# Group norm on quarters of the PE array, and row sums of the spatial weights by halves

## The chip, the cores and the metric

The kernel runs on one core of one Trainium2 chip. The metric is the device time of one execution in microseconds (us). The kernel before took 996.74 us (median of three runs, 996.4 to 1000.49). The engines are named as in the profile: PE multiplies matrices (its weight loads are PEld), DVE is the vector engine, ACT the scalar engine, POOL the GpSimd engine and SP the engine that issues the DMAs. PE's clock has two levels, 1.2 and 2.4 GHz; a granted clock of 1.00 in a row is the upper one.

## The reference

The reference is one decoder block on 1024 tokens of width 1024. Two mixers stand side by side, a spatial gating unit (A) and a convolution branch (B), and a dense feed-forward part follows:

```
z = rmsnorm(x) modulated @ w_in + b_in;   u, v, val, gate = split(z)
y_a = gelu(u) * (tril(w_s) applied along each chunk of 128 tokens to layernorm(gelu(v)) + b_s)
y = depthwise causal conv, width 31, of val * sigmoid(gate), + bias
y_b = silu(layernorm of y over each of 8 groups of 64 channels, scaled by gn_g, shifted by gn_b)
x = x + gate1 * (concat(rmsnorm(y_a), rmsnorm(y_b)) @ w_out)
x = x + gate2 * ((silu(h2 @ wg) * (h2 @ wu)) @ w_ffn_out);   out = rmsnorm(x) modulated
```

The change touches the layer norm of branch B, called group norm below, and one term of branch A: since layernorm(v) has a shift, w_s applied to it needs the sum of each row of w_s times that shift, which the kernel folds into the bias b_s.

## The kernel before

Everything is held transposed: channels on the 128 partitions, tokens along the free axis, in two halves of 512 tokens. Most products are three matmuls (`mm3`, lines L603 to L605; `L928` in the feed-forward part): each operand is split into a high and a low part, and hi*hi, lo*hi and hi*lo are added in PSUM. The stages come in this order: norm of the first token half and adaLN; the gated projections `p` of half 0; `pu` and `v`; the spatial mixing `pm`; group norm of half 0; the same for half 1; the output projection `po`; then the feed-forward part in three rounds (`ah`, B and C banks) up to about 972 us; last the final norm and the output.

At the start, the squares `sq_n` are summed over channels by matmuls with 32 columns (`ssq_n`, L648: four of them, one for each quarter of the tokens), c is spread to all partitions (`c`, L538, two matmuls from one partition), silu of it is `cact` (L539), and DVE multiplies rows of the adaLN weights by `cact` and sums them (L559, on tiles called `ypad`, later `ada`) to get columns of `cond`. ACT finishes those columns (L722, L723); the first tile of activations is `t_h` on DVE (L725), `t_h` on ACT (L726), and `h` on ACT (L728, high part). The first gated product `p` (L603) needs `h`.

Group norm (`group_norm`, L881 on) runs four times, for two token halves times two pairs of channel tiles; each is called (half, pair) below, (0,0) to (1,1). A channel tile has 128 channels, so two groups of 64. Each run has these steps:
- L886: one fp32 matmul of 128 rows by 128 columns by 512 tokens for each tile, with the matrix `gcen` (identity less the mean over 64 channels), takes the mean away. `gcen` has nothing but zeros in two of its four quarters.
- L889, L890: ACT squares the result (`gsq`) and copies it back to `s`.
- L893: eight matmuls of 32 columns sum the squares by groups, for a quarter of the tokens (128) each, into one bank.
- L896, L897: ACT takes the root, DVE the reciprocal (`gsd`).
- L901: sixteen matmuls of 64 columns and 128 rows spread the factors over the channels.
- L904, L905: DVE multiplies, ACT applies silu with scale and shift.

The row sums of the spatial weights (`spatial_bias`, L698) are two fp32 matmuls against ones with 512 columns each, and eight DVE instructions (L707) on 64 partitions and 128 columns that add them into `bst`.

The order of all instructions on each engine is not the program's own: `fix_order` (L452) gives a list scheduler the whole program. It has a table of durations (`duration`, L125), a graph of dependences (`Graph`) and a simple clock of the engines (`Clock`, L313), which adds 0.09 and 0.12 us whenever PE goes to matmuls on a part of the array and back. It plans forward and backward a few times, takes the plan with the shortest modelled span, and fixes each engine's sequence. So a changed duration or a changed count of matmuls can move work anywhere in the program.

## Time and profile before

| | before |
|---|---|
| runs | 996.4, 996.74, 1000.49 us (median 996.74) |
| the profiled execution | 996.41 us, span in the trace 994.4 us |
| mean granted PE clock | 0.995 |
| PE busy | 961.9 us, 97% of the span, 4645 instructions |
| DVE busy | 855.2 us, 86% |
| ACT, POOL busy | 474.0 us (48%), 391.4 us (39%) |
| chain that ended last | PE 83%, DVE 10% |

The span runs from the first to the last instruction; the device time has 2.0 us beside it. A share of the span says how long an engine had work, not whether that work is on the chain that ends last; for this the windows and the timelines have to be read stage by stage. A PE matmul record lasts longer than its distance from the next one, since matmuls are pipelined: the cost of a matmul is read from start to start. A plain matmul of 512 columns starts 0.227 us after the one before. An fp32 matmul shows as two records.

### The profile page before, as it was taken

To read this page: it belongs to the slowest core of one execution; us is meant where nothing else is said; L and a number is where in the kernel's file an instruction comes from. 1 tells how busy PE (TensorE), PEld (TensorE's weight loads), DVE (VectorE), ACT (ScalarE), POOL (GpSimd) and SP (SyncE) were. 2 spreads that over 40 slices of the span, in tenths; PEclk is the share of its full clock that TensorE was granted. 3 is DMA by queue.
4 is the path that set the end of the run, shared out by engine and by line. 5 is a ranking of instruction groups with operands and counts; after the bars stand their busy time and mean duration, and the time that the engine had idled before them with its cause. 6 is when DMAs were issued, how large, how long until landed. Compare 5 with 4: busy or idle time off the path is not lost.

```text
span 994.4 us, 13218 instructions
## 1 busy us (share of the span) xinstructions
PE 961.9 (97%) x4645; PEld 773.6 (78%) x4645; DVE 855.2 (86%) x1197; ACT 474.0 (48%) x751; POOL 391.4 (39%) x232
## 2 busy tenths in 40 slices
PE   4999999999999999999999999999999999999994
PEld 2887777778878778888888877888887888888873
DVE  3969999999999444799999999998678989869946
ACT  6668467643484363564332332323337437236416
POOL 0037879755556111574445544445443100000121
PEclk9999999999999999999999999999999999999997
DMA  8983351524465515764677777677557838315104
GB/s 301 329 315 101 123 175 56 189 96 127 148 223 180 190 43 169 259 232 145 221 253 233 244 240 255 227 241 234 186 180 259 303 131 259 121 40 173 33 1 169
DMA packets 73667, 184.08 MB, mean 185 GB/s; under 512 B 8193, under 2 KB 10497, under 8 KB 73602
## 3 DMA queue, kind: packets, MB, share of 16 engines
q1 hardware_dynamic: 73602, 183.25, 55.6%
q8 instruction: 36, 0.59, 0.3%
q14 instruction: 29, 0.24, 0.1%
HBM read 142.06 MB, written 41.16 MB: 184 GB/s over the span
## 4 chain that ended last, share of the span: by engine, by line
PE 83%; DVE 10%; issue 2%; ACT 2%; DMA 1%; POOL 0%; SPq 0%; ACTq 0%; DVEq 0%; POOLq 0%
PE B L928 24%; PE C L928 14%; PE ah L928 11%; PE p L603 3%; PE po L603 3%; PE po L604 3%; PE po L605 3%; PE p L604 3%; PE p L605 3%; PE A L928 3%; DVE w_f L921 2%; PE v L604 2%; PE v L603 1%; PE pu L605 1%; PE v L605 1%
## 5 line engine op out<-in xcount | busy, mean ns | idle before, releaser
L928 PE MATMUL B<-h,w_f 128*128 128x512 f32 x816 | 190.8, 390 | 2.3 <-ACT x L1145 1.2
L928 PEld LDWEIGHTS B<-h,w_f 128*128 128x128 f32 x816 | 152.7, 188 | 36.4 <-DVE x L1147 3.1
L866 DVE SCALAR_TENSOR_TENSOR cv<-ypad,colt,cv 128x512 f32<-128x512 f32 x216 | 147.6, 745 | 0.5
L928 PE MATMUL B<-fa,w_d 128*128 128x512 f32 x528 | 125.5, 390 | 0.3 <-DVE x L1277 0.2
L928 PE MATMUL C<-h,w_f 128*128 128x512 f32 x528 | 123.6, 389 | 0.0
L928 PEld LDWEIGHTS B<-fa,w_d 128*128 128x128 f32 x528 | 98.8, 188 | 22.0 <-DVE x L1277 1.1
L928 PEld LDWEIGHTS C<-h,w_f 128*128 128x128 f32 x528 | 99.1, 188 | 20.6
L928 PE MATMUL ah<-h,wh_a 128*128 128x512 f32 x320 | 101.6, 395 | 0.5 <-ACT sg L673 0.5
L1209 POOL TENSOR_TENSOR sq_nf<-sq_nf,sq_nf 128x512 f32<-128x512 f32 x9 | 12.5, 1388 | 175.6 <-ACT sq_nf L1204 175.6
L920 ACT ACTIVATE w_d<-raw_d 128x512 fp32r<-128x512 f32 (+1 forms) x72 | 42.0, 593 | 83.0 <-PE B L928 34.0
L1170 POOL TENSOR_TENSOR x<-x,up 128x512 f32<-128x512 f32 x20 | 34.7, 1737 | 106.1 <-ACT x L1169 106.1
L587 POOL TENSOR_TENSOR wl_a<-raw_a,wh_a 128x1024 fp32r<-128x1024 f32 x20 | 49.2, 2461 | 67.8 <-ACT wh_a L586 57.7
L920 ACT ACTIVATE w_f<-raw_f 128x512 fp32r<-128x512 f32 x68 | 42.3, 627 | 68.4 <-PE B L928 41.6
L921 DVE TENSOR_TENSOR w_f<-raw_f,w_f 128x512 fp32r<-128x512 f32 x68 | 68.7, 1017 | 5.1 <-ACT w_f L920 5.0
L928 PEld LDWEIGHTS ah<-h,wh_a 128*128 128x128 f32 x320 | 59.9, 188 | 15.1 <-issue 1.4
L928 PE MATMUL C<-fa,w_d 128*128 128x512 f32 (+1 forms) x273 | 64.4, 384 | 0.0
L928 PE MATMUL ah<-h,wl_a 128*128 128x512 f32 x160 | 62.2, 390 | 0.0
L928 PEld LDWEIGHTS C<-fa,w_d 128*128 128x128 f32 x273 | 49.9, 188 | 11.0 <-issue 0.8
L921 DVE TENSOR_TENSOR fa<-a,fa 128x512 fp32r<-128x512 f32 x77 | 54.2, 743 | 1.7 <-ACT fa L920 1.7
L1277 DVE SCALAR_TENSOR_TENSOR x<-B,cond,x 128x512 f32<-128x512 f32 x48 | 35.6, 743 | 19.8 <-PE B L928 19.8
L920 ACT ACTIVATE fa<-a 128x512 fp32r<-128x512 f32 x77 | 46.0, 626 | 8.8 <-DMA a<-acts 5.7
L921 DVE TENSOR_TENSOR w_d<-raw_d,w_d 128x512 fp32r<-128x512 f32 (+1 forms) x72 | 47.8, 673 | 1.4 <-ACT w_d L920 1.4
(236 smaller groups left out, 2094.2 us busy)
## 6 DMA issues: line engine op xcount, KB each, us to landing
acts<-x SPq DMA_DIRECT2D x77, 256.0 KB, 3.1
a<-acts SPq DMA_DIRECT2D x77, 256.0 KB, 4.0
raw_f<-wf SPq DMA_DIRECT2D x32, 512.0 KB, 4.5
ada<-ada SPq DMA_DIRECT2D x24, 512.0 KB, 3.4
x<-ada SPq DMA_DIRECT2D x24, 512.0 KB, 3.8
raw_a<-wf SPq DMA_DIRECT2D x20, 512.0 KB, 3.8
ahead<-ahead SPq DMA_DIRECT2D x40, 256.0 KB, 3.0
ypad<-ada SPq DMA_DIRECT2D x16, 512.0 KB, 5.4
```

The lines of the kernel that those rows point to most:

```text
L587: lo_eng.tensor_tensor(lo, raw, hi.bitcast(F32), op=ALU.subtract)
L603: PE.matmul(acc, shi, mhi, start=start, stop=False)
L604: PE.matmul(acc, slo, mhi, start=False, stop=False)
L605: PE.matmul(acc, shi, mlo, start=False, stop=stop)
L866: V.scalar_tensor_tensor(accs[j], src, wc, accs[j], op0=ALU.mult, op1=ALU.add)
L920: A.activation(dst[:, 0, :], src, AF.Copy)
L921: lo_eng.tensor_tensor(dst[:, 1, :], src, dst[:, 0, :].bitcast(F32), op=ALU.subtract)
L928: last_mm = PE.matmul(bank[:, cols], s, m[:, cols], start=first and p == 0 and i == 0, stop=p == n - 1 and i == 2, skip_group_check=True)
L1170: G.tensor_tensor(g0, g0, up0, op=ALU.mult)
L1209: G.tensor_tensor(sums[half], sums[half], t, op=ALU.add)
L1277: V.scalar_tensor_tensor(xs[k][:, part], bank[:, cols], ccol(GATE2, k), xs[k][:, part], op0=ALU.mult, op1=ALU.add)
```

## The change

What the change does:
- L886: `gcen` is applied by its quarters. Each tile's matmul becomes two, each with 64 rows and 64 columns. The first tile's go on the two quarters of the array on the diagonal; the second tile's on the other two, so that its two halves of 64 channels come out exchanged. On the host the tables that belong to the second tile (group norm's scale and shift, the norm's gain, rows of `w_out`) are exchanged in the same way.
- L893: same number of matmuls; the layout of the sums in the bank is another, with each tile's sums on its own 64 partitions, and the order of the loop is another.
- L901: the sixteen spreading matmuls have 64 rows in place of 128, and their loop alternates between the two tiles.
- `spatial_bias`: two matmuls become eight of 64 columns and 128 tokens in one bank, and eight DVE instructions become four on 128 partitions.
- The planner: durations of an fp32 matmul in proportion to its columns and half as long with up to 64 rows; the matmuls of one PSUM bank stay in order; the clock of the forward plan runs PE at half speed when the stretch before was little used.

```
-            for hh in range(4):
...
+        rs = mm_bank("rs")
+        for hp in range(4):
+            for e in range(2):
+                PE.matmul(rs[e * 64:(e + 1) * 64, hp * P:(hp + 1) * P], ones.broadcast_to([P, 64]),
+                          wt[:, 2 * hp + e, :], start=True, stop=True)
+        for hp in range(4):
+            V.scalar_tensor_tensor(bst[:, hp, :], rs[:, hp * P:(hp + 1) * P], col("a_ln_b", hp),
+                                   bst[:, hp, :], op0=ALU.mult, op1=ALU.add)
...
-        for j in js:
-            PE.matmul(bank[j], gcen, s[j], start=True, stop=True)
+        for row in range(2):
+            for i, j in enumerate(js):
+                rows, outs = slice(row * 64, row * 64 + 64), slice((row ^ i) * 64, (row ^ i) * 64 + 64)
+                PE.matmul(bank[j][outs], gcen[rows, rows], s[j][rows], start=True, stop=True)
...
-        for i, j in enumerate(js):
-            for q in range(4):
-                PE.matmul(b0[q * 32:(q + 1) * 32, 0:P], gind[:, 32 * i:32 * i + 32],
-                          sqs[j][:, q * P:(q + 1) * P], start=i == 0, stop=i == 1)
+        for e in range(2):
+            for i, j in enumerate(js):
+                for b in range(2):
+                    o, q = 64 * i + 32 * b, 2 * b + e
+                    PE.matmul(b0[o:o + 32, 0:P], gind[:, 32 * e:32 * e + 32],
+                              sqs[j][:, q * P:(q + 1) * P], start=e == 0, stop=e == 1)
...
-        for i, (j, b) in enumerate(zip(js, (b1, b0))):
-            for q in range(4):
+        for q in range(4):
+            for i, b in enumerate((b1, b0)):
+                rows = slice(64 * i, 64 * i + 64)
                 for g in range(2):
                     PE.matmul(b[g * 64:(g + 1) * 64, q * P:(q + 1) * P],
-                              col("sel_grp", 8 * i + 2 * q + g).broadcast_to([P, 64]), sd,
+                              col("sel_grp", 2 * q + g)[rows].broadcast_to([64, 64]), sd[rows],
                               start=True, stop=True)
...
-        elif n == 128:
-            t = {128: 0.219, 32: 0.068}.get(m, 0.109)
         else:
-            t = 0.857
+            k = s.reads[0].box[1] - s.reads[0].box[0]
+            t = {128: 0.219, 32: 0.068}.get(m, 0.109 if k > 64 else 0.055) * n / 128
...
+            if s.engine == "PE":
+                if s.writes[0].name in bank:
+                    s.before.add(bank[s.writes[0].name])
+                bank[s.writes[0].name] = s.n
...
+        slow = 2 if self.throttled and self.active.get(w - 1, 0.0) < CLOCK_WINDOW / 2 else 1
```

What moves, at three places. In these rows a name ends in the number of its tile, and x2 or x4 counts equal instructions in a row; lines of the changed kernel are some 20 higher.

**The start.** PE of the kernel before, from the fifth sum of squares to the first two products:

```order
L648 MATMUL ssq_n1_0_119<-sq_n1_0_3_138,ones_92 32x128 x4
L648 MATMUL ssq_n1_0_119<-sq_n1_0_4_144,ones_92 32x128 x4
L538 MATMUL c0_97<-c_row_72,ones_92 128x512
L648 MATMUL ssq_n1_0_119<-sq_n1_0_5_150,ones_92 32x128 x4
L538 MATMUL c1_100<-c_row_72,ones_92 128x512
L648 MATMUL ssq_n1_0_119<-sq_n1_0_6_156,ones_92 32x128 x4
L648 MATMUL ssq_n1_0_119<-sq_n1_0_7_162,ones_92 32x128 x4
L654 MATMUL ssq_n1_0_119<-rt_n1_0_168,colt_74 128x128 x4
```

PE of the changed kernel at the same place:

```order
L669 MATMUL ssq_n1_0_119<-sq_n1_0_3_138,ones_92 32x128 x2
L559 MATMUL c0_97<-c_row_72,ones_92 128x512
L669 MATMUL ssq_n1_0_119<-sq_n1_0_3_138,ones_92 32x128 x2
L669 MATMUL ssq_n1_0_119<-sq_n1_0_4_144,ones_92 32x128 x4
L669 MATMUL ssq_n1_0_119<-sq_n1_0_5_150,ones_92 32x128 x4
L669 MATMUL ssq_n1_0_119<-sq_n1_0_6_156,ones_92 32x128 x4
L559 MATMUL c1_100<-c_row_72,ones_92 128x512
L669 MATMUL ssq_n1_0_119<-sq_n1_0_7_162,ones_92 32x128 x4
L675 MATMUL ssq_n1_0_119<-rt_n1_0_168,colt_74 128x128 x4
```

One more sum of squares (`sq_n1_0_6`) stands ahead of the second `c`, and the first `c` is two and a half sums earlier. ACT of the kernel before, from the first norm factor `r_n` on (`cond` with `gain` is L722, without it L723):

```order
L660 ACTIVATE r_n1_0_175<-ssq_n1_0_119 128x512
L722 ACTIVATE cond_105<-cond_105,gain_185,colt_74 128x1
L726 ACTIVATE t_h1_0_0_199<-t_h1_0_0_199,cond_105 128x512
L586 ACTIVATE wh_k1_235<-raw_k1_233 128x1024
L728 ACTIVATE h1_0_0_202<-t_h1_0_0_199 128x512
L723 ACTIVATE cond_105<-cond_105,colt_74 128x1
L726 ACTIVATE t_h1_0_1_241<-t_h1_0_1_241,cond_105 128x512
```

ACT of the changed kernel:

```order
L681 ACTIVATE r_n1_0_175<-ssq_n1_0_119 128x512
L741 ACTIVATE cond_105<-cond_105,gain_185,colt_74 128x1
L742 ACTIVATE cond_105<-cond_105,colt_74 128x1
L607 ACTIVATE wh_k1_235<-raw_k1_233 128x1024
L745 ACTIVATE t_h1_0_0_199<-t_h1_0_0_199,cond_105 128x512
L745 ACTIVATE t_h1_0_1_241<-t_h1_0_1_241,cond_105 128x512
L747 ACTIVATE h1_0_0_202<-t_h1_0_0_199 128x512
```

The second `cond` column, the next weights `wh_k1` and the second tile's `t_h` now all stand ahead of `h1_0_0`. DVE of the kernel before at that time:

```order
L559 SCALAR_TENSOR_TENSOR ypad2_108,cond_105<-ypad2_108,cact_96 128x1024
L725 TENSOR_TENSOR t_h1_0_0_199<-x0_76,r_n1_0_175 128x512
L559 SCALAR_TENSOR_TENSOR ypad3_109,cond_105<-ypad3_109,cact_96 128x1024
L725 TENSOR_TENSOR t_h1_0_1_241<-x1_77,r_n1_0_175 128x512
L725 TENSOR_TENSOR t_h1_0_2_283<-x2_78,r_n1_0_175 128x512
L729 TENSOR_TENSOR h1_0_0_202<-t_h1_0_0_199,h1_0_0_202 128x512
```

DVE of the changed kernel:

```order
L580 SCALAR_TENSOR_TENSOR ypad2_108,cond_105<-ypad2_108,cact_96 128x1024
L580 SCALAR_TENSOR_TENSOR ypad3_109,cond_105<-ypad3_109,cact_96 128x1024
L744 TENSOR_TENSOR t_h1_0_0_199<-x0_76,r_n1_0_175 128x512
L744 TENSOR_TENSOR t_h1_0_1_241<-x1_77,r_n1_0_175 128x512
L744 TENSOR_TENSOR t_h1_0_2_283<-x2_78,r_n1_0_175 128x512
L608 TENSOR_TENSOR wl_k1_236<-raw_k1_233,wh_k1_235 128x1024
L748 TENSOR_TENSOR h1_0_0_202<-t_h1_0_0_199,h1_0_0_202 128x512
```

The fourth `ypad` stands ahead of the first `t_h` where it stood behind it.

**Group norm (0,1).** PE of the kernel before, at the centring of the second pair of tiles (`gn0_2`, `gn0_3`):

```order
L605 MATMUL p11_0_1776<-h1_1_0_791,wh_vg11_0_1768 128x512
L603 MATMUL p11_0_1776<-h1_1_1_797,wh_vg11_0_1768 128x512
L886 MATMUL gn0_2_1553<-s0_2_1141,cstt_118 128x512
L886 MATMUL gn0_3_1554<-s0_3_1142,cstt_118 128x512
L604 MATMUL p11_0_1776<-h1_1_1_797,wl_vg11_0_1769 128x512
L605 MATMUL p11_0_1776<-h1_1_1_797,wh_vg11_0_1768 128x512
L603 MATMUL p11_0_1776<-h1_1_2_803,wh_vg11_0_1768 128x512
L893 MATMUL gn0_2_1553<-gsq0_2_1557,cstt_118 32x128 x4
L604 MATMUL p11_0_1776<-h1_1_2_803,wl_vg11_0_1769 128x512
L893 MATMUL gn0_2_1553<-gsq0_3_1560,cstt_118 32x128 x4
L605 MATMUL p11_0_1776<-h1_1_2_803,wh_vg11_0_1768 128x512
L603 MATMUL p11_0_1776<-h1_1_3_809,wh_vg11_0_1768 128x512
```

PE of the changed kernel (L907 is the centring, L916 the sums by groups, L787 the last matmul of `v`, L669 a sum of squares):

```order
L626 MATMUL v1_3_1429<-wl_v_3_992,h1_1_7_833 128x512
L907 MATMUL gn0_2_1556<-s0_2_1142,cstt_118 64x512 x2
L787 MATMUL v1_3_1429<-vb_116,vsel_117 128x512
L624 MATMUL p10_0_1746<-h1_1_0_791,wh_vg10_0_1738 128x512
L669 MATMUL ssq_a0_1599<-sq_a0_0_1600,ones_92 32x128 x4
L625 MATMUL p10_0_1746<-h1_1_0_791,wl_vg10_0_1739 128x512
L907 MATMUL gn0_3_1557<-s0_3_1143,cstt_118 64x512 x2
L626 MATMUL p10_0_1746<-h1_1_0_791,wh_vg10_0_1738 128x512
L624 MATMUL p10_0_1746<-h1_1_1_797,wh_vg10_0_1738 128x512
L916 MATMUL gn0_2_1556<-gsq0_2_1562,cstt_118 32x128 x2
L625 MATMUL p10_0_1746<-h1_1_1_797,wl_vg10_0_1739 128x512
L626 MATMUL p10_0_1746<-h1_1_1_797,wh_vg10_0_1738 128x512
```

The centring stands about 33 plain matmuls earlier, and its two pairs of quarters are no longer next to each other. In (0,0) all eight pieces are together and the spreading alternates between the tiles; in (1,0) the four quarters are together, and the spreading comes in two parts; in (1,1) the quarters are in two parts, and the spreading does one tile after the other. Counted over the program, PE goes to a block of matmuls on a part of the array 46 times where it went 37 times: group norm 19 for 11, row sums 1 for none, `pm` 6 for 7, the final norm 7 for 6.

**The end.** DVE of the kernel before (`x3` are the last products added to x, `rt_nf` the factors of the final norm, `of` output tiles):

```order
L1277 SCALAR_TENSOR_TENSOR x3_79<-C2_3_8208,cond_105,x3_79 128x256
L1244 SCALAR_TENSOR_TENSOR of0_4_8237<-x4_80,cond_105,ssq_nf0_8003 128x512
L1277 SCALAR_TENSOR_TENSOR x3_79<-C2_3_8208,cond_105,x3_79 128x256
L1226 RECIPROCAL rt_nf1_8269<-rt_nf1_8269 64x128
L1226 RECIPROCAL rt_nf2_8274<-rt_nf2_8274 64x128
L1244 SCALAR_TENSOR_TENSOR of0_6_8289<-x6_82,cond_105,ssq_nf0_8003 128x512
```

DVE of the changed kernel:

```order
L1302 SCALAR_TENSOR_TENSOR x3_79<-C2_3_8217,cond_105,x3_79 128x256
L1269 SCALAR_TENSOR_TENSOR of0_2_8242<-x2_78,cond_105,ssq_nf0_8012 128x512
L1269 SCALAR_TENSOR_TENSOR of0_4_8246<-x4_80,cond_105,ssq_nf0_8012 128x512
L1251 RECIPROCAL rt_nf1_8278<-rt_nf1_8278 64x128
L1302 SCALAR_TENSOR_TENSOR x3_79<-C2_3_8217,cond_105,x3_79 128x256
L1251 RECIPROCAL rt_nf2_8283<-rt_nf2_8283 64x128
L1269 SCALAR_TENSOR_TENSOR of0_6_8298<-x6_82,cond_105,ssq_nf0_8012 128x512
```

The first of the two reciprocals now stands ahead of the last product of `x3` where it stood behind it.

## Rows read from the trace of the kernel before

**Rows 1.** From the profile's page: busy time of PE and DVE, and the shares of the chain that ended last.
```profile
PE 961.9 (97%) x4645; PEld 773.6 (78%) x4645; DVE 855.2 (86%) x1197; ACT 474.0 (48%) x751; POOL 391.4 (39%) x232
...
PE 83%; DVE 10%; issue 2%; ACT 2%; DMA 1%; POOL 0%; SPq 0%; ACTq 0%; DVEq 0%; POOLq 0%
```
**Rows 2.** Busy time by stretches of the span: stretch, length, then for PE, PEld, DVE, ACT and POOL the busy us and instructions, the granted PE clock, DMA share, GB/s.
```profile
25.00:50.00 25.00, 25.00 (x106) 20.53 (x105) 25.00 (x38) 16.50 (x28) 0.00 (x0) 1.00 0.93 329
...
250.00:275.00 25.00, 25.00 (x134) 20.04 (x133) 24.62 (x36) 11.06 (x15) 13.91 (x7) 1.00 0.47 155
...
500.00:600.00 100.00, 99.81 (x438) 81.66 (x437) 99.98 (x127) 31.01 (x51) 49.68 (x29) 1.00 0.76 247
```
**Rows 3.** Timeline of PE at the start: start us, length, line, operation, shape, count [idle before, ended by].
```profile
8.57 1.30 PE L648 MATMUL ssq_n<-sq_n,ones 128*32 128x128 f32 x16 [1.59 <-ACT sq_n L641]
9.80 2.07 PE L538 MATMUL c<-c_row,ones 1*128 1x512 f32 x2
11.80 0.66 PE L648 MATMUL ssq_n<-sq_n,ones 128*32 128x128 f32 x8
12.39 2.07 PE L538 MATMUL c<-c_row,ones 1*128 1x512 f32 x2
...
24.22 0.80 PE L603 MATMUL p<-h,wh_k 128*128 128x512 f32 x1 [3.72 <-ACT h L728]
...
25.25 0.63 PE L603 MATMUL p<-h,wh_k 128*128 128x512 f32 x1
25.67 0.63 PE L604 MATMUL p<-h,wl_k 128*128 128x512 f32 x1
```
**Rows 4.** Timeline of ACT at the start.
```profile
21.89 0.81 ACT L726 ACTIVATE t_h<-t_h,cond 128x512 f32<-128x512 f32 x1 [0.29 <-DVE t_h L725]
22.61 1.04 ACT L586 ACTIVATE wh_k<-raw_k 128x1024 fp32r<-128x1024 f32 x1
23.56 0.61 ACT L728 ACTIVATE h<-t_h 128x512 fp32r<-128x512 f32 x1
24.08 0.28 ACT L723 ACTIVATE cond<-cond,colt 128x1 f32<-128x1 f32 x1
```
**Rows 5.** Timeline of DVE at the start.
```profile
19.95 1.22 DVE L559 SCALAR_TENSOR_TENSOR ypad<-ypad,cact 128x1024 f32<-128x1024 f32 x1
...
21.16 0.69 DVE L725 TENSOR_TENSOR t_h<-x,r_n 128x512 f32<-128x512 f32 x1
21.78 1.22 DVE L559 SCALAR_TENSOR_TENSOR ypad<-ypad,cact 128x1024 f32<-128x1024 f32 x1
```
**Rows 6.** Timeline of PE at the centring of (0,0): one plain matmul, the two fp32 matmuls of 128 by 128 by 512 (four records), and two plain ones, of which the first is left out.
```profile
141.66 0.39 PE L768 MATMUL v<-vb,vsel 128*128 128x512 f32 x1
141.90 1.88 PE L886 MATMUL gn<-s,cstt 128*128 128x512 f32 x4
...
143.85 0.40 PE L604 MATMUL v<-wh_v,h 128*128 128x512 f32 x1
```
**Rows 7.** Timeline of PE at the sums by groups of (0,0), eight matmuls of 32 columns (16 records) between plain ones, of which the first behind the block is left out.
```profile
144.08 0.40 PE L605 MATMUL v<-wl_v,h 128*128 128x512 f32 x1
144.41 0.64 PE L893 MATMUL gn<-gsq,cstt 128*32 128x128 f32 x16
...
145.32 0.40 PE L604 MATMUL v<-wh_v,h 128*128 128x512 f32 x1
```
**Rows 8.** Timeline of PE at the spreading of (0,0), sixteen matmuls of 64 columns in one block (32 records), and of (0,1), the first eight of them; the plain matmul right behind each block is left out.
```profile
153.06 0.39 PE L604 MATMUL v<-wh_v,h 128*128 128x512 f32 x1
153.38 1.97 PE L901 MATMUL gn<-gsd,colt 128*64 128x128 f32 x32
...
155.62 0.40 PE L603 MATMUL v<-wh_v,h 128*128 128x512 f32 x1
...
187.44 0.39 PE L604 MATMUL p<-h,wl_vg 128*128 128x512 f32 x1
187.76 1.09 PE L901 MATMUL gn<-gsd,colt 128*64 128x128 f32 x16
...
189.12 0.40 PE L603 MATMUL p<-h,wh_vg 128*128 128x512 f32 x1
```
**Rows 9.** Timelines at the row sums: PE's two fp32 matmuls between plain ones (the first one behind them is left out), then DVE's eight instructions.
```profile
117.13 0.39 PE L605 MATMUL pu<-h,wh_u 128*128 128x512 f32 x1
117.36 1.88 PE L702 MATMUL rs<-wt,ones 128*128 128x512 f32 x4
...
119.35 0.39 PE L604 MATMUL v<-wh_v,h 128*128 128x512 f32 x1
...
119.08 2.91 DVE L707 SCALAR_TENSOR_TENSOR bst<-rs,colt,bst 64x128 f32<-64x128 f32 x8
```
**Rows 10.** Timeline of DVE at the adding up for (0,1), the last step before its centring.
```profile
173.45 1.28 DVE L875 TENSOR_TENSOR s<-s,cv 128x512 f32<-128x512 f32 x2
```
**Rows 11.** Timeline of DVE at the end.
```profile
978.17 0.48 DVE L1277 SCALAR_TENSOR_TENSOR x<-C,cond,x 128x256 f32<-128x256 f32 x1 [1.17 <-PE C L928]
978.92 0.94 DVE L1226 RECIPROCAL rt_nf<-rt_nf 64x128 f32<-64x128 f32 x1 [0.26 <-ACT rt_nf L1225]
980.10 0.94 DVE L1226 RECIPROCAL rt_nf<-rt_nf 64x128 f32<-64x128 f32 x1 [0.24 <-ACT rt_nf L1225]
980.97 4.92 DVE L1244 SCALAR_TENSOR_TENSOR of<-x,cond,ssq_nf 128x512 f32<-128x512 f32 x11
```

More of the change, by code (lines that the diff above doesn't have):

```diff
@@ L176, in __init__ @@
         self.steps = []
-        uses, live, tiles, order = {}, {}, {}, {}
+        uses, live, tiles, order, bank = {}, {}, {}, {}, {}
         for ins in instructions:
@@ L319, in __init__, with tensor @@
         self.last, self.partial = None, False
+        self.throttled, self.active = throttled, {}
+    def tensor(self, t, s):
+        if s.partial != self.partial:
+            self.partial = s.partial
+            t += 0.09 if s.partial else 0.12
+        w = int(t / CLOCK_WINDOW)
+        slow = 2 if self.throttled and self.active.get(w - 1, 0.0) < CLOCK_WINDOW / 2 else 1
+        end = t + slow * s.issue
+        a = t
+        while a < end:
+            w = int(a / CLOCK_WINDOW + 1e-9)
+            b = min(end, (w + 1) * CLOCK_WINDOW)
+            self.active[w] = self.active.get(w, 0.0) + b - a
+            a = b
+        self.free["PE"] = end
+        return t, t + slow * s.finish
     def run(self, s, t):
@@ L405, in forward @@
             same = g.steps[n].engine == e and not s.dma
-            at[n] = max(at[n], (begin + s.issue if e == "PE" else end) if same else end + SIGNAL[e])
+            at[n] = max(at[n], (clock.free[e] if e == "PE" else end) if same else end + SIGNAL[e])
             if not need[n]:
@@ L1377 @@
     gind = np.zeros((P, 2, 32))
[L1378 to L1379 removed]
+    sel_grp = np.zeros((2, 2, 32, 4, 2))
+    for e in range(2):
         for g in range(2):
[L1381 to L1384 removed]
+            gind[part // 64 == g, e, 2 * e + g] = 1.0 / 64
+            for b in range(2):
+                sel_grp[:, b, 2 * e + g, 2 * b + e, g] = 1.0
+    colv.update(sel_tok=part[:, None] == 32 * np.arange(4)[None, :], sel_grp=sel_grp.reshape(P, 8),
                 sel_hl=((part == 0) | (part == 32))[:, None])
```

41 lines of the change are left out of this document (17 added, 24 removed).

## The prediction

> **What bounds the kernel now.** I read the page first. PE is busy 97% of the span and holds 83% of the chain that ended last; DVE holds 10% [rows 1]. Then the windows: in each of the ten stretches of 25 us from 25 to 275 us, whose first and last are shown, PE has no idle time (25.00 of 25.00), while DVE is full in some stretches only; between 500 and 600 us DVE is the fuller one, 99.98 to 99.81 [rows 2]. All that the change edits lies before 375 us: the row sums at 117, group norm at 142 to 190 and at 280 to 356. There every microsecond that PE needs more or less moves all that follows, and DVE's full stretch in the feed-forward part starts from results of PE, so it moves along. The two ends are latency: PE waits 3.7 us for the first `h` at 24.22 [rows 3], and the last DVE and output chain runs with PE idle [rows 11]. So the sum is made of PE's time in the edited blocks, and of shifts on the two ends. DVE's saving is left out of it, for the reason below.
>
> **Prices on PE.** They are read start to start, less 0.227 for each plain matmul in between. The two full centring matmuls cost 143.85 - 141.66 - 2 x 0.227 = 1.74, so 0.87 each [rows 6]. The eight group sums cost 145.32 - 144.08 - 0.45 = 0.79 [rows 7]. Sixteen spreading matmuls in one block cost 155.62 - 153.06 - 0.45 = 2.11, eight alone 189.12 - 187.44 - 0.45 = 1.23 [rows 8]. In a spreading block two matmuls of 64 columns run beside each other, one on each half of the columns; the second eight therefore add 0.88, about 0.11 for each matmul, and a visit to a block costs 1.23 - 0.88 = 0.35 beyond its matmuls. The group sums run four beside each other, so 0.79 is 0.35 and about 0.44. A visit thus costs 0.35, and this is paid for every block that the order makes, even a small one. Full matmuls like the old centring do not pay it.
>
> What no row shows is two matmuls on different halves of the rows beside each other. From below: they overlap in full, as column halves do; from above: one waits for the other. I take overlap, since the nearest rows are those of column tiles, and keep the other end as a rival.
>
> **Part by part, on PE, with overlap.**
> - Row sums: before 119.35 - 117.13 - 0.45 = 1.77 [rows 9]. After, eight matmuls of 64 columns with 128 rows are the half block of rows 8, so 1.23: -0.54.
> - (0,0), where the order keeps the four quarters together: centring 1.74 becomes one visit and one full length, 0.35 + 0.87 = 1.22. Group sums are now two blocks of two and six, 0.35 + 0.22 and 0.35 + 0.44 = 1.36 for 0.79. Spreading puts four beside each other: 0.35 + 0.88 = 1.23 for 2.11. Together 3.81 for 4.64: -0.8.
> - (0,1): centring in two blocks, 2 x 1.22 = 2.44 for 1.74; sums 1.36 for two blocks of 0.57 each, 1.14; spreading two blocks of eight as before, 2.46. Together 6.26 for 5.34: +0.9.
> - (1,0): centring 1.22 for 1.74, sums and spreading as before: -0.5.
> - (1,1): centring 2.44 for 1.74; sums 1.36 for 0.79; spreading does one tile after the other, so the row halves do not meet: 2.11 as before. +1.3.
> - One `pm` block fewer: -0.35.
>
> The sum is -0.54 - 0.8 + 0.9 - 0.5 + 1.3 - 0.35 = 0.0. What the quarters give in (0,0) and (1,0), the extra visits take in (0,1) and (1,1).
>
> **DVE.** Eight instructions of 2.91 us [rows 9] become four on twice the partitions, about 1.45. PE is full there and waits for nothing of DVE's, so this is worth nothing in time. It moves the adding up for (0,1) forward by about 1.5 us and a bit more from other orders, from 174.7 (173.45 + 1.28) [rows 10] to some 173. The centring that waits for it, however, is 33 plain matmuls earlier: 180.47 less 33 x 0.227 is 173. These two meet; a wait of 0 to 1 us is possible there, and behind it on PE all of the first `p` of the second half is queued. I take 0.
>
> **The start.** Ahead of the second `c` there is one more sum of squares, 0.6 us (11.80 to 12.39) [rows 3]: `c` starts at about 13.0, and all on DVE behind `cact` is 0.6 later, the third `ypad` at 20.55 instead of 19.95. One `ypad` takes 1.2 from start to start (19.95 to 21.16); the third and the fourth are now both ahead of the first `t_h`, which so starts at 22.95 rather than 21.16 [rows 5]. ACT now does the second `cond` column, which needs that `ypad`, then `wh_k1`, then two `t_h`, then `h`: 22.97 + 0.28 + 0.95 + 0.72 + 0.72 = 25.64, where `h` started at 23.56 [rows 4]. The first product follows 0.66 later, at 26.3 rather than 24.22 [rows 3]: +2.1. PE runs without a gap from here to 275 us [rows 2], so nothing takes this back. Cover for it could come only from matmuls that run faster: the first products start 0.43 apart (25.25 to 25.67) [rows 3], not 0.227, which is the pace of the lower of the two clock levels; that slow stretch begins with the first product, so I count it as moved as a whole. Bounds: 0 if the scheduled steps are not late in fact, 2.5 if a weight is late too.
>
> **The end.** DVE does the first reciprocal (0.87 start to start) ahead of the last product of `x3`. PE gives the sum that it needs 5 of 9 matmuls earlier, some 0.6, so the reciprocal starts at about 978.3 and the product at 979.2 in place of 978.17; from there the chain to the first output tile is the same (980.97 - 978.17 = 2.8), less 0.1 to 0.2 of a wait for ACT that falls away [rows 11]. The output chain starts 0.9 us later: +0.9, bounds 0 and 1.1.
>
> **Sum.** The profiled execution took 996.41 us (span 994.4, 2.0 beside it), the median of the runs 996.74. 996.4 + 0.0 + 0 + 2.1 + 0.9 = 999.4. That is 0.3% above the median, and by less than what can be told from no change.
>
> **A rule against it.** The rows show only matmuls on all rows or alone [rows 6 to 8], so none shows two row halves. The Trainium skill, page "TensorEngine Tiling (Array Packing)", section "Restrictions and Gotchas", says that tiles on different rows cannot access the same PSUM bank at the same time. No run before shows this. In (0,0) and (1,1) the first two quarters of a tile are on different rows and go to one bank, which is what the next rival takes up as a mechanism.
>
> **Rivals.**
> - *Row halves do not run beside each other (slower).* The place is L886 in all four runs and the spreading of (0,0). If the second quarter of a tile waits for the first one, each centring that is one full length above becomes two, in (0,0) four: 3 x 0.87 + 2 x 0.87 + 1 x 0.87 + 2 x 0.87 = 7.0, and the spreading of (0,0) 0.88 more; 999.4 + 7.9 = 1007. If only quarters that share a bank wait, (0,0) has three lengths and the spreading is spared: 2 + 2 + 1 + 2 = 7 lengths of 0.87, 6.1, so 1005.5. It decides from 2.3 us on, where the sum passes 1001.7. For it: no row shows the overlap. Against: column halves overlap in every block. Chance 0.2.
> - *The centring of (0,1) and the steps behind it wait (slower).* The order was made for a clock that is not the chip's; where DVE's adding up for (0,1) ends after PE is there, PE waits, and all of the first `p` behind it; up to 1 us there, and as much at each of the three steps behind it that hang on the same chain (sums, root, spreading): 1000.4 to 1003.4. For it: rows 10 and the meeting times above. Against: DVE gains 1.5 us. Chance 0.15.
> - *The quarters pay in full (faster).* The gain would be that of (0,0) in all four, 4 x 0.9 = 3.6 with 0.5 from row sums, and the start not late because the order shifts it back: 996.4 - 4 = 992.3; with gains in the rest of the order 989 to 992. For it: order of the feed-forward part also changes and its small PE waits can go. Against: the blocks are split in two runs, by the order. Chance 0.1.
> - *The change moves nothing.* The start and the end are as before in fact; 995.5 to 997. Chance 0.1.
>
> **How the numbers follow.** My forecast (997 to 1001.5) has 0.45. A change within 0.5% cannot be told from none here, that is 991.8 to 1001.7. Same: 0.45 + 0.1 (moves nothing) + 0.08 of the waits, which lie on both sides of 1001.7, + 0.04 of the full gain = 0.67. Slower: 0.2 + 0.07 of the waits = 0.27. Faster: the rest of the full gain, 0.06. The range leaves out the gains in full (0.1) and the upper part of the slower rival (0.08): 995 to 1006.5. Only the likeliest case alone: 997 to 1001.5.
>
> **What would show each step.** In the profile of the changed kernel: the first `p` at about 26.3 us, with `h` the releaser (start). The centring of (0,0) with four records started nearly together, and 1.2 us for the block (overlap); starts 0.43 apart pass after pass say that row halves wait. The spreading of (0,0) at 1.2 us with four records to a step. Blocks of two quarters in (0,1) at 1.2 us each. A wait of PE for `s` from DVE at the centring of (0,1). The first `of` of the last group about 1 us further from the last plain matmul. Wrong would be: a first `p` before 25.5, or a feed-forward part whose length differs by more than 1 us.

## The result and the profile after

The changed kernel took 999.75 us (median of 20 runs, 998.08 to 1002.63) beside 996.82 us for the kernel before (20 runs); the ratio is 1.0022, 95% interval 1.0012 to 1.0032. The forecast of 999.4 us held in its number. The slowdown of 0.1 to 0.3% lies inside the 0.5% that the prediction counted as no change, though over 20 runs it is clear of none. What follows shows that terms it did not have, of opposite sign, lie behind that number as well.

The page of the changed kernel's profile (profiled execution 1001.04 us, span 999.3, granted clock 0.992) has PE busy for 963.2 us, 96% of the span, and this chain, as in [rows 1]:

```profile
PE 87%; DVE 4%; ACT 3%; DMA 2%; issue 2%; POOL 1%; SPq 0%; ACTq 0%; DVEq 0%; POOLq 0%
```

**The start.** Timeline of PE, as [rows 3]:

```profile
9.78 2.07 PE L559 MATMUL c<-c_row,ones 1*128 1x512 f32 x2
11.78 1.92 PE L669 MATMUL ssq_n<-sq_n,ones 128*32 128x128 f32 x28
13.63 2.07 PE L559 MATMUL c<-c_row,ones 1*128 1x512 f32 x2
...
26.83 0.79 PE L624 MATMUL p<-h,wh_k 128*128 128x512 f32 x1 [5.09 <-ACT h L747]
```

of ACT, as [rows 4]:

```profile
23.60 0.29 ACT L742 ACTIVATE cond<-cond,colt 128x1 f32<-128x1 f32 x1 [0.76 <-DVE ypad L580]
23.80 1.04 ACT L607 ACTIVATE wh_k<-raw_k 128x1024 fp32r<-128x1024 f32 x1
24.75 1.50 ACT L745 ACTIVATE t_h<-t_h,cond 128x512 f32<-128x512 f32 x2
26.16 1.14 ACT L747 ACTIVATE h<-t_h 128x512 fp32r<-128x512 f32 x2
```

and of DVE, as [rows 5]:

```profile
22.34 1.22 DVE L580 SCALAR_TENSOR_TENSOR ypad<-ypad,cact 128x1024 f32<-128x1024 f32 x1
...
23.49 1.89 DVE L744 TENSOR_TENSOR t_h<-x,r_n 128x512 f32<-128x512 f32 x3
```

The chain is the predicted one, link by link: ACT waits 0.76 us for the fourth `ypad`, then come `cond`, the weights, two `t_h` and `h`. The wait for `h` grew from 3.72 to 5.09 us, by 1.37 where the sum had 1.5, and the first product starts at 26.83. The second `c`, though, starts 1.24 us later than before (13.63 for 12.39), not 0.6: between the two `c` there are now three and a half sums of squares (28 records, 8 before), and the first `c` starts no earlier than before (9.78 for 9.80), although two and a half sums fewer stand ahead of it.

**The blocks of group norm.** Timeline of PE: centring and spreading of (0,0), as [rows 6, 8], then the first of the two centring blocks of (0,1), and the spreading of (1,1):

```profile
145.37 0.40 PE L787 MATMUL v<-vb,vsel 128*128 128x512 f32 x1
145.70 1.09 PE L907 MATMUL gn<-s,cstt 64*64 64x512 f32 x8
146.72 0.50 PE L624 MATMUL v<-wh_v,h 128*128 128x512 f32 x1
147.05 0.40 PE L625 MATMUL v<-wh_v,h 128*128 128x512 f32 x1
...
155.04 0.39 PE L626 MATMUL v<-wl_v,h 128*128 128x512 f32 x1
155.36 1.10 PE L925 MATMUL gn<-gsd,colt 64*64 64x128 f32 x32
...
156.73 0.40 PE L625 MATMUL v<-wh_v,h 128*128 128x512 f32 x1
...
176.03 0.39 PE L626 MATMUL v<-wl_v,h 128*128 128x512 f32 x1
176.35 1.08 PE L907 MATMUL gn<-s,cstt 64*64 64x512 f32 x4
177.35 0.49 PE L787 MATMUL v<-vb,vsel 128*128 128x512 f32 x1
177.69 0.39 PE L624 MATMUL p<-h,wh_vg 128*128 128x512 f32 x1
...
358.27 0.39 PE L625 MATMUL po<-y_a,wl_o 128*128 128x512 f32 x1
358.59 1.59 PE L925 MATMUL gn<-gsd,colt 64*64 64x128 f32 x32
...
360.44 0.39 PE L624 MATMUL po<-y_a,wh_o 128*128 128x512 f32 x1
```

Read start to start, less two plain matmuls (0.45): eight records of four quarters cost 147.05 - 145.37 - 0.45 = 1.23 us, four records of two quarters 177.69 - 176.03 - 0.45 = 1.21, and 32 records of the spreading 156.73 - 155.04 - 0.45 = 1.24; in (1,1), where one tile follows the other, 360.44 - 358.27 - 0.45 = 1.72. Two quarters cost as much as four. This is what the prediction expects of row halves that run beside each other; experiment 5 takes up what else it could be.

**The end.** Timeline of DVE, as [rows 11]:

```profile
982.36 0.94 DVE L1251 RECIPROCAL rt_nf<-rt_nf 64x128 f32<-64x128 f32 x1 [1.04 <-ACT rt_nf L1250]
983.23 0.38 DVE L1302 SCALAR_TENSOR_TENSOR x<-C,cond,x 128x256 f32<-128x256 f32 x1
...
985.90 4.91 DVE L1269 SCALAR_TENSOR_TENSOR of<-x,cond,ssq_nf 128x512 f32<-128x512 f32 x11
```

The last product of `x3` stands behind the reciprocal and starts 0.87 later than that. It starts 0.80 us behind the last `C` product on PE (982.43), where it started 0.31 behind it before (977.86 and 978.17 in [rows 11]), and the output tiles 3.47 for 3.11: some 0.4 us. The other part of the end stands on PE: from the last `B` to the last `C` product it takes 12.53 us for 12.00, with a block of sums for the final norm (four records at 981.51) between the last `C` products, where it stood behind them.

**What the prediction did not have.** The table of PE's waits of the changed kernel (us in total, times, longest), some of its rows:

```profile
PE pu L624 <- ACT h L641: 1.3, 1, 1.3
PE ah L953 <- ACT sg L694: 1.2, 1, 1.2
PE B L953 <- DVE x L1172: 0.9, 2, 0.5
```

and the same table of the kernel before:

```profile
PE B L928 <- ACT x L1145: 1.2, 1, 1.2
PE B L928 <- DVE x L1147: 0.9, 1, 0.9
...
PE ah L928 <- ACT sg L673: 0.5, 1, 0.5
PE B L928 <- DVE x L1277: 0.2, 1, 0.2
```

The wait in `pu` is new; in the feed-forward part waits have gone. Where the first comes from is seen on the timelines of PE, DVE and ACT of the changed kernel, rows of all three in order of time:

```profile
95.66 0.39 PE L626 MATMUL pu<-h,wh_u 128*128 128x512 f32 x1
95.89 1.05 PE L675 MATMUL ssq_n<-rt_n,colt 128*128 128x128 f32 x8
96.98 0.75 DVE L636 SCALAR_TENSOR_TENSOR t_h<-x,cond,ssq_n 128x512 f32<-128x512 f32 x1 [0.92 <-PE ssq_n L675]
97.76 0.72 ACT L640 ACTIVATE t_h<-t_h,cond 128x512 f32<-128x512 f32 x1 [3.49 <-DVE t_h L636]
98.39 0.67 ACT L818 ACTIVATE ya<-pu,colt 128x512 f32<-128x512 f32 x1
98.96 0.62 ACT L641 ACTIVATE h<-t_h 128x512 fp32r<-128x512 f32 x1
99.63 0.50 PE L624 MATMUL pu<-h,wh_u 128*128 128x512 f32 x1 [1.30 <-ACT h L641]
```

PE spreads the norm factors of the second half (`ssq_n`) behind 26 products of `pu` in a row, and only six products stand behind it until the first that needs the new `h`. These cover 1.4 us, while `t_h`, another activation of ACT (`ya`) and `h` take 2.6 from the end of `ssq_n`. On DVE eight steps of the convolution stand ahead of the reciprocal that `ssq_n` needs, where three stood before, and it starts at 93.89 us for 90.52. But it is done at 94.83, and in this trace `ssq_n` follows the last product without a wait; in two later traces of this kernel it comes some 0.3 us late. So the order on PE and ACT makes most of this wait.

### The profile page after: what moved, and what is told of

Read it like the earlier page. It is cut to its first block, busy times and chain, and to the rows that moved or that the text cites. A ratio compares the mean times of both kernels' runs of the same rounds, so it can differ in the third digit from the quotient of the medians.

```text
span 999.3 us, 13264 instructions
## 1 busy us (share of the span) xinstructions
PE 963.2 (96%) x4673; PEld 773.2 (77%) x4673; DVE 862.6 (86%) x1193; ACT 476.4 (48%) x751; POOL 396.5 (40%) x232
## 4 chain that ended last, share of the span: by engine, by line
PE 87%; DVE 4%; ACT 3%; DMA 2%; issue 2%; POOL 1%; SPq 0%; ACTq 0%; DVEq 0%; POOLq 0%
PE B L953 28%; PE C L953 16%; PE ah L953 11%; PE A L953 3%; PE po L624 3%; PE po L625 3%; PE po L626 3%; PE p L624 2%; PE p L626 2%; PE p L625 2%; PE v L624 2%; PE v L626 2%; PE pu L624 1%; PE v L625 1%; PE pu L625 1%
## 5 line engine op out<-in xcount | busy, mean ns | idle before, releaser
L945 ACT ACTIVATE w_f<-raw_f 128x512 fp32r<-128x512 f32 x68 | 42.3, 628 | 72.3 <-PE B L953 39.5
```

Of the source, the lines that this page charges most:

```text
L945: A.activation(dst[:, 0, :], src, AF.Copy)
```

## Experiments

All ratios are to the kernel before, run beside them. Where the order of all else is said to be the same, every engine has the same sequence but for the instructions named.

**1. The planner's clock undone.**

```
-    slots, clock, table = Slots(g), Clock(True), None
+    slots, clock, table = Slots(g), Clock(), None
```

> The changed kernel with one line of the planner undone: its clock no longer runs PE at half speed after a little used stretch; everything else as changed. The order that comes out has the start and the end of the kernel before, the quarters of (0,1) in one block, the spreading of (0,1) in one block, and four pm blocks for six. My theory (PE blocks priced by visits, late start +2.1, late end +0.9, both from that one line): first product near 24.2 us, PE blocks 2.3 us cheaper than before the change (row sums -0.54, (0,0) -0.8, (0,1) -0.65, (1,0) -0.5, (1,1) +1.3, pm -1.05), so 994.5 us, ratio to before 0.998. Rival 1 (the group norm's own edits cost the time, the start is only noise of the DMA landing): 999 or more. Rival 2 (what is gained before 400 us is given back in the feed-forward part, where DVE is full): 996.5 to 997.

Measured 997.6 us (11 runs), ratio 1.000 (0.999 to 1.001). The late start and the late end are gone: PE waits 3.7 us for the first `h` as before, and from the last C product to the end of the span it takes 16.55 us, as before (16.57), where the changed kernel has 16.90. So in the changed kernel that one line makes the wait for `h` longer and the end late. It does not do so in every order: experiments 2 and 3 keep the line and have the wait of 5.1 us, but the end of before (16.6 and 16.5 us), and first products at 24.99 and 24.44, since their second `c` is not late. Added up on PE's timeline between plain matmuls, all blocks of fp32 matmuls up to the last one of group norm cost 38.7 us for 42.3 before, 3.6 less where the theory had 2.3. The time is 3 us above my theory's, and near rival 2's number, but from the first to the last B product this trace takes 516.0 us, not more than the 517.7 of before. Its trace has lost the rest ahead of the feed-forward part: PE waits 1.0 us for `sg` in `p` and a second time for `rt_n`, 1.4 us (a wait that one later trace of the kernel before has as well), and the clock fell after the wait for `y_b`, which experiments 7 and 8 take up.

**2. The planner's part alone**, with group norm and the row sums of the kernel before.

```
+            k = s.reads[0].box[1] - s.reads[0].box[0]
+            t = {128: 0.219, 32: 0.068}.get(m, 0.109 if k > 64 else 0.055) * n / 128
...
+                    s.before.add(bank[s.writes[0].name])
...
+    slots, clock, table = Slots(g), Clock(True), None
```

> The kernel before with only the planner's part of the change (durations, bank order, half-speed clock); group norm and row sums untouched. The order has the late start (fourth ypad ahead of the first t_h, two t_h ahead of h) but the second c where it was, and the end as before. My theory: first product +1.5 us, two pm blocks fewer and one group norm block more (-0.35), so 998.0, ratio 1.001. Rival 1 (the edits of group norm cost the time): 996.8. Rival 2 (the orders of the feed-forward part differ by more than all this): anything from 994 to 1001 with the first product at +1.5.

Measured 999.36 us (10 runs, 997.94 to 1004.8), ratio 1.0038 (1.0022 to 1.0054). The planner alone makes the kernel slower. The interval overlaps that of the whole change (1.0012 to 1.0032), so that the edits in group norm and the row sums give some of it back is not shown, and the edits under the old planner were not run. In its trace PE waits 5.09 us for the first `h`, as with the whole change, and the first product is at 24.99, +1.0 for the expected +1.5; ahead of the last group norm it has further waits, 1.2 us for `sg` in `pu`, 1.6 for a square `sq_n` and 0.5 for `s` in `pm`.

**3. The steps of group norm held together in blocks** (nine of the twelve in one, three still split once). Planner edges let the four quarters wait for both tiles and the eight sums for both squares, and hold the matmuls of a step in their own order:

```
+    def together(mms, ready=None):
+        edges.extend((m.name, ready.name) for m in mms if ready is not None)
+        edges.extend((b.name, a.name) for a, b in zip(mms, mms[1:]))
```

> The changed kernel with planner edges that make each group norm's four quarters wait for both tiles, its eight sums wait for both squares, and the spreading keep its alternating order, so that each step is one block in all four runs (three of the twelve are still split once). Planner's half-speed clock kept; the two c stand together early, so that the first product should come near 24.2. My theory: a step costs 1.22, 0.79 and 1.23 in one block, 3.24 a run for 4.6 to 5.3 before, with three splits at 0.35: PE blocks 6.5 us below the kernel before, so 990.3, ratio 0.9935. Rival 1 (visits are not the price, or the waits for the second tile take the place of what is saved): 997 to 999. Rival 2 (DVE's full stretch takes the gain back): 993 to 995.

Measured 993.09 us (6 runs), ratio 0.9962 (0.9948 to 0.9976). The direction held, the size did not: 3.9 us were gained of 6.5. The number is rival 2's, but not its mechanism: from the first to the last B product the trace takes 517.8 us, as before. In the trace the spreading of (1,1), which does one tile after the other in the changed kernel, is one block of four quarters at a time:

```profile
351.33 0.39 PE L625 MATMUL po<-y_a,wl_o 128*128 128x512 f32 x1
351.65 1.10 PE L934 MATMUL gn<-gsd,colt 64*64 64x128 f32 x32
...
353.02 0.40 PE L624 MATMUL po<-y_a,wh_o 128*128 128x512 f32 x1
```

353.02 - 351.33 - 0.45 = 1.24 us, and with the table further down: from the first product to the last matmul of group norm 328.0 us, for about 331.0 before, so 3 of the 6.5 us. The blocks themselves (group norm, row sums and `pm`, added up on PE's timeline) cost 26.6 us for 31.9, 5.3 less. Of that, waits for other engines take some: PE waits 1.5 us for `rt_b` where it waited 0.6, and 1.2 for `sg` where it waited 0.5. Where the rest goes is not shown.

**4. The same with the planner's clock undone.**

> As the gathered kernel, and with the planner's clock of the kernel before, so that the start and the end are those of before and pm has four blocks. My theory: PE blocks 7.2 us below the kernel before: 989.6, ratio 0.9928. Rival 1 (visits not the price): 996 to 997. Rival 2 (gain taken back by DVE's full stretch): 993 to 995.

Measured 994.85 us (12 runs), ratio 0.9974 (0.9962 to 0.9987): in rival 2's range, and not better than experiment 3. Here too the trace does not show rival 2's mechanism (517.1 us from the first to the last B product). All blocks of fp32 matmuls up to the last one of group norm cost 35.7 us for 42.3, 6.6 less; new waits take part of it, 1.7 us for `sg` in `p` and 1.5 for `rt_b` where it was 0.6, and in the profiled execution the clock fell behind the wait for `y_b`.

**5. The gathered kernel without the exchange of halves.**

```
-                rows, outs = slice(row * 64, row * 64 + 64), slice((row ^ i) * 64, (row ^ i) * 64 + 64)
+                rows, outs = slice(row * 64, row * 64 + 64), slice(row * 64, row * 64 + 64)
...
-        v = np.stack([v[:, 0], v[:, 1, ::-1]], axis=1).reshape((n * P,) + v.shape[4:])
+        v = np.stack([v[:, 0], v[:, 1]], axis=1).reshape((n * P,) + v.shape[4:])
```

> The gathered kernel with the second tile's halves not exchanged: both tiles' quarters lie on the diagonal of the array, and the tables on the host are left in their own order. The order of every engine's instructions is the same as in the gathered kernel. My theory (quarters run beside each other only where they are different quarters of the array): the first tile's quarter blocks the second's, the third quarter joins the second, so each centring block takes two to three lengths of 0.87 where it took one: 2.1 to 2.95 us for 1.22 in the trace, four times, so 3.5 to 7 us more on PE, of which some is given back later: 996 to 999 (gathered kernel 993.1). Rival (the four matmuls of a block were never beside each other, the gain came from the planner's order): same time, block length unchanged.

Measured 997.63 us (12 runs), ratio 0.999 (0.9974 to 1.0006) where the exchange gives 0.9962. Its centring block in (0,0):

```profile
142.39 0.40 PE L787 MATMUL v<-vb,vsel 128*128 128x512 f32 x1
142.72 1.94 PE L912 MATMUL gn<-s,cstt 64*64 64x512 f32 x8
...
144.93 0.39 PE L625 MATMUL v<-wh_v,h 128*128 128x512 f32 x1
```

144.93 - 142.39 - 0.45 = 2.09 us for 1.23 with the exchange: one length of 0.87 more, four times, 3.4 us. The same order of all instructions rules out that the order made the difference.

Two lengths, not three: in the program's order the second matmul of the block needs the quarter of the first, and the third a free one. If each started only after the one before it had, there would be three lengths, 2.96 us; so the third did not wait for the second.

One rival gives the same sums. If a matmul on 64 rows took half as long, as the planner's table now has it, and the row halves came one after the other, two quarters and four would cost 0.35 + 2 x 0.43 = 1.2 us, and the block without the exchange 0.35 + 4 x 0.43 = 2.1. The gathered kernel's trace decides: the centring of (1,1) is split there, one quarter alone (two records), then three.

```profile
342.93 1.07 PE L912 MATMUL gn<-s,cstt 64*64 64x512 f32 x2
343.92 0.50 PE L963 MATMUL ah<-h,wh_a 128*128 128x512 f32 x1
344.36 1.08 PE L912 MATMUL gn<-s,cstt 64*64 64x512 f32 x6
345.37 0.50 PE L963 MATMUL ah<-h,wh_a 128*128 128x512 f32 x1
```

From the start of the block to the next plain matmul it takes 0.99 us with one quarter and 1.01 with three, as it takes 1.00 with two (176.35 to 177.35) and 1.02 with four (145.70 to 146.72) in the changed kernel. One quarter takes the whole length, so the row halves do run beside each other. Quarters run beside each other only where they are different quarters.

**6. A known delay ahead of the feed-forward part.** In the kernel before, order of all else the same:

```
+            if half == 1 and ns == (7,):
+                for _ in range(22):
+                    EXTRA.add(PE.matmul(banks[7], unit(ws[7], 0)[0], full(yl[0])[0], start=True, stop=False,
+                                        skip_group_check=True).ins.name)
```

> The kernel before with 22 plain matmuls (22 x 0.227 = 5.0 us) added on PE just ahead of the last output projection of the second token half, at about 390 us; their results are overwritten by the next matmul, and the order of all other instructions on every engine is that of before. My theory after the first four runs (lateness at 409 us is given back in part by the feed-forward part, since about 0.28 of it was gone by 950 us in the five traces so far): +3.6 us at the end, 1000.5. Rival (the feed-forward part shifts as a whole, as the prediction had it; the differences between the traces came from other orders there): +5.0, 1002. Rival 2 (DVE's stretch does not depend on PE at all): +1 to +2.

Measured 1002.06 us (12 runs), ratio 1.0045 (1.003 to 1.006), so 3.0 to 6.0 us later. The first B product starts 4.97 us later than in the first trace of before, the last C product 5.68 later. The interval holds the theory's 3.6 as well as the rival's 5.0, so the times do not tell them apart. The trace speaks for the rival: from the first to the last B product it takes 518.4 us, inside the 517.6 to 519.5 of the other traces of before. The feed-forward part moves as a whole, as the prediction had it, as far as one trace can show; that it gives back 4 of 5 us is excluded.

**7. Zero matmuls in PE's wait for `y_b`**, in the changed kernel, order of all else the same but for the instruction that makes the zero:

```
+                    if half == 1 and part == 1 and n == 0:
+                        for _ in range(6):
+                            m = PE.matmul(banks[0], zero.broadcast_to([P, P]), full(yl[0])[0], start=False,
+                                          stop=False, skip_group_check=True).ins
...
```

> The changed kernel with six plain matmuls with a zero stationary operand (nothing is added to the result), in PE's wait of 1.57 us for y_b at 370 us; all other orders are the same but for one small ACT instruction at the start that makes the zero. In the changed kernel's trace the granted clock fell to 0.67 in 370 to 375 after that wait, and the po matmuls ran 0.43 apart; before the change it stayed at 1.00. Theory: with PE busy in the wait the clock stays at 1.00, po at 380 us comes 1.5 us earlier, the end about 1.1 earlier: 998.6. Rival (the fall has another cause, or it differs from run to run): the clock falls again, 999.7.

Measured 999.55 us (12 runs), ratio 1.0015 (1.000 to 1.003), not to be told from the 1.0022 without. The granted clock did stay at 1.00. The window of 365 to 375 us (PE busy, granted clock, DMA share, GB/s) in the changed kernel:

```profile
365.00:375.00 10.00, 7.62 (x35) 0.83 0.00 0
```

and in the one with the wait filled:

```profile
365.00:375.00 10.00, 9.01 (x48) 1.00 0.00 0
```

whose timeline of PE there is:

```profile
369.72 1.64 PE L947 MATMUL po<-y_a,zero 128*128 128x512 f32 x6
371.54 0.50 PE L631 MATMUL po<-y_b,wh_o 128*128 128x512 f32 x1 [0.18 <-ACT y_b L850]
```

In this trace the last `po` is 1.5 us earlier than in that of the changed kernel (406.90 for 408.40). The next run bears on why the median gains little: without filler, too, the clock does not fall every time.

**8. The kernel before again.**

> The kernel before once more, for a second trace: how far the landmarks move between two executions of one program (first product at 24.2, last product of the feed-forward part at 978). If the input's landing at the start or the clock after the wait at 366 us differ by 0.5 us or more here, differences of that size between other traces are no effect of the change. Expected: first product 24.2 to 24.9, clock 1.00 after the wait, 996 to 998.

Measured 1000.03 us in one run. The same order, the same wait of 1.50 us, and this time the clock falls, as the same window and the timeline of PE behind the wait show:

```profile
365.00:375.00 10.00, 8.50 (x33) 0.83 0.00 0
```

```profile
366.85 0.70 PE L603 MATMUL po<-y_b,wh_o 128*128 128x512 f32 x1 [1.50 <-ACT y_b L824]
367.35 0.63 PE L604 MATMUL po<-y_b,wl_o 128*128 128x512 f32 x1
367.78 0.63 PE L603 MATMUL po<-y_b,wh_o 128*128 128x512 f32 x1
```

The products start 0.43 apart, the pace of the lower of the two levels, and the landmarks behind are 1.6 us later. So this is no effect of the change: both kernels have it in some executions. Of the ten traces of this document in which PE waits 1.5 to 1.6 us for `y_b` without filler, the clock fell behind the wait in five.

**9. The gathered kernel with the wait filled** (the edits of 3 and 7).

> The gathered kernel with the six zero matmuls of the filled-wait kernel in PE's wait for y_b; the order of all else is that of the gathered kernel. Theory: blocks as in the gathered kernel (about 4 us below the kernel before), and the granted clock after the wait stays at 1.00 in every execution, where it fell in some of those without filler: ratio to before 0.9955 to 0.996, and a smaller spread of the single runs. Rival: the filler has no effect on the median, 0.9962 as without.

Measured 991.99 us (6 runs, 991.81 to 994.65), ratio 0.9961 (0.9948 to 0.9973). It beats both kernels, and is no better than experiment 3 by what can be told. In its trace the clock stayed at 1.00 behind the wait; with experiment 7 these are two traces, too few to show that the filler keeps it there.

**10 and 11. Both kernels again.**

> The changed kernel once more, for a second trace of the same order. Stage lengths to compare with the traces of before (three so far, 517.7, 519.5 and 518.4 us from the first B product to the last): if the changed kernel's feed-forward order is faster by itself, that length is again near 515 (515.2 and 514.4 in its two traces so far); if those were chance, 517 to 519. First product at 26.2 to 26.9, PE's wait for h in pu near 1.3 us, clock after the wait for y_b 1.00 or about 0.7, ratio 1.002 to 1.003.

> The kernel before a third time, beside the changed kernel in the same call: first B to last B product 517.5 to 519.5 us if its feed-forward order is slower by itself, near 515 if the length differs by chance. First product 23.9 to 24.9, 995 to 1000 us.

Measured 998.9 us (9 runs), ratio 1.0024 (1.0013 to 1.0035), for the changed kernel, and 998.08 in one run for the one before. The starts of five landmarks on PE and the end of the span, in us:

| trace | first p | last of group norm | first B | last B | last C | end |
|---|---|---|---|---|---|---|
| before | 24.22 | 355.08 | 448.22 | 965.87 | 977.86 | 994.43 |
| before again (8) | 23.93 | 355.29 | 450.01 | 969.51 | 981.51 | 998.08 |
| before again (11) | 23.73 | 356.91 | 450.10 | 967.65 | 979.64 | 996.22 |
| before and delay (6) | 24.21 | 355.01 | 453.19 | 971.55 | 983.54 | 1000.11 |
| changed | 26.83 | 359.91 | 454.71 | 969.90 | 982.43 | 999.33 |
| changed again (10) | 26.30 | 360.39 | 453.66 | 966.77 | 979.30 | 996.20 |
| changed, filled (7) | 26.35 | 359.89 | 453.18 | 967.61 | 980.13 | 997.82 |
| gathered (3) | 24.44 | 352.48 | 445.50 | 963.26 | 975.26 | 991.78 |

From first to last B the order of before takes 517.7, 519.5, 517.6 and 518.4 us, the changed order 515.2, 513.1 and 514.4. The same number of matmuls stands between the two landmarks. Within one order the length moves by some 2 us (the gathered kernel and experiment 5 have one order, and take 517.8 and 515.6), but the two sets do not touch, and side by side, in experiments 10 and 11, they are 4.4 us apart: the feed-forward part of the changed order is some 4.0 us shorter by itself (means 518.3 and 514.2). Experiment 6 shows that this is not because it starts later: 5 us later, the order of before still takes 518.4.

## Why the prediction was right, point by point

- **Blocks on PE (predicted 0.0 in all).** The prices hold to a few hundredths: one visit and one length 1.23 for 1.22, the spreading of (0,0) 1.24 for 1.23, two quarters alone 1.21. One was too high: two tiles' spreading one after the other in (1,1) cost 1.72, not 2.11, so the row halves meet in part there. Added up on PE's timeline between plain matmuls, group norm, row sums and `pm` cost 31.3 us for 31.9 before, so -0.6 for the predicted 0.0.
- **Row halves beside each other.** The step that no row of before showed, and the rival that hung on it, are settled by the blocks above and by experiment 5 with the single quarter shown there: they run beside each other, and matmuls on the same quarter do not. The rule of the Trainium skill that the prediction weighed (page "TensorEngine Tiling (Array Packing)", section "Restrictions and Gotchas": tiles on different rows can't access one PSUM bank at the same time) does not agree: in (0,1) two quarters on different rows write different partitions of one bank, and the block takes 1.21 us, not 2.1. The measurement decides.
- **The start (predicted +2.1).** Measured: the means of the first product are 24.02 (four traces of before's order) and 26.49 (three of the changed order), so +2.5. The links are those that were named; mis-sized was the second `c`, 1.24 us late in the first trace for 0.6. Experiment 1 shows that the planner's clock is the cause of the longer wait for `h`; how late `c` comes is another matter of the order (experiments 2 and 3). The first products start 0.43 apart in the traces of both kernels, so the slow stretch did move along, as the prediction took it.
- **The end (predicted +0.9).** Last B to last C 12.53 us for 12.00, and last C to the end 16.90 for 16.57, so +0.86 in two of the three traces; in the third, that of experiment 7, the last C to the end takes 17.69. The number fits, the reason in part: the reciprocal gives some 0.4 of it. The other 0.5 is the added block of the final norm on PE (7 for 6 in the count of blocks), which the sum left out, though it had a price for it, 0.35.
- **"PE runs without a gap from here to 275 us, so nothing takes this back."** This failed. The changed order itself has a gap there, 1.30 us in `pu`, since six products cover the 2.6 us until the second half's first `h` only in part. I had read the windows of before, and not looked for what the new order puts around the second half's norm. With 0.7 more for `sg` in `ah` that is +2.0 that the sum did not have. From the first product to the last matmul of group norm the changed kernel takes 333.6 us (mean of three), the one before 331.0 (its three traces without the one that waits 1.6 us for `rt_n` a second time; 331.5 with it): +2.6 or +2.0.
- **The centring of (0,1) waits (a rival, 0.15).** It did not: the changed kernel's table of waits has no wait of PE for `s` there, and 176.35 follows 176.03 as in the other blocks.
- **"DVE's full stretch moves along."** As to lateness this was right (experiment 6). But the sum took the feed-forward part's order as equal, and it was 4.0 us shorter: a term that I set to zero without costing it. The prediction had named a length that differs by more than 1 us as a sign that it is wrong, and by this sign it is. In the four traces of the order of before, the waits of B for `x` and of C for `fa` add up to 2.3, 4.3, 2.8 and 3.3 us; in the three of the changed order to 0.9, 0.3 and 0.9. That is 2.5 of the 4.0. Which step on DVE made them shorter I have not shown.

Together, with +0.2 from the last matmul of group norm to the first B: +2.5 + 2.6 + 0.2 - 4.0 + 0.5 + 0.6 = +2.4 by the means of the traces (+1.8 with all four of the order of before; the delay of experiment 6 is taken off), beside +2.9 and +1.9 in two sets of medians. The number of the forecast, +2.6 to 3.0, came out because the missed terms, +2.0 and -4.0, and the 0.4 by which the start was short, cancel in good part. The prices of the blocks, the links of the start and half of the end were right; that the middle came to no more than this was not reasoned, and was luck.

## What to carry to other kernels

Pricing a block of small matmuls needs two numbers, its lengths and the visits (0.35 us each here): an edit that halves the lengths and lets a scheduler split the blocks comes out even, and the same edit with the blocks held together gave 0.4%. When a planner writes the order, a changed cost model is an edit of its own, and must be timed alone (here 1.0038); what it does far from the edited code, on the engine that feeds the bounding one, has to be read with the same care as the edited place. And before a difference of one or two us between two traces is explained, the same kernel has to be traced again.

## What was not expected of the hardware

- The granted clock after a PE wait of 1.5 us fell to 0.83 over 10 us in one execution of a kernel and stayed at 1.00 in another with the same order and the same wait, which is worth 1.6 us each time. It fell in five of ten traces with such a wait. With the wait filled by zero matmuls it stayed at 1.00 in both traces of kernels that had them; that the filler is the reason is not shown.
- Two quarters that write different partitions of one PSUM bank from different rows cost no more than one: from the start of the block to the next plain matmul 0.99 us for one, 1.00 for two and 1.02 for four.
- Sixteen matmuls of 64 rows and columns cost 1.24 us with the row halves in turn and 1.72 with one row half after the other, so PE starts some of the second half's before the first half's are done. In the centring without the exchange (2.09 us for four matmuls on two quarters) a matmul on a free quarter did not wait for an earlier one whose quarter was busy.
